# Unused full-width products beside the small products of the inverses' joining and of the sample sequences

## The chip, the cores and the metric

One Trainium2 chip, one of its cores. The metric is the device time of one execution in microseconds (us). The kernel before took 1914.19 us, the median of three runs (1911.26 to 1918.53).

## The reference

One inference step of a one-layer hybrid decoder trunk: 1024 prompt tokens and 8 sample sequences of 8 tokens, model width 1024. What matters here is the first of three parallel head groups, the RWKV-7 time mixing (8 heads of 64), a recurrence over tokens with a 64x64 state per head:

```python
def step(S, inp):
    r_t, w_t, k_t, v_t, a_t, b_t = inp
    sa = jnp.einsum('bhij,bhj->bhi', S, a_t)
    S = (S * w_t[:, :, None, :] + sa[..., None] * b_t[:, :, None, :]
         + v_t[..., None] * k_t[:, :, None, :])
    return S, jnp.einsum('bhij,bhj->bhi', S, r_t)
...
x = x + jnp.concatenate([y_a, y_b, y_c], axis=-1) @ w_out[l]
x = x + mem_attend(rms_norm(x, norm_mem_q[l]), mem_ks[l], mem_vs[l], mem_wq[l], mem_wo[l])
x = x + swiglu(rms_norm(x, norm_ffn[l]), ffn_w_up[l], ffn_w_down[l])
```

The other two head groups are a gated linear recurrence (RG-LRU) and a diagonal state-space model (S5). Everything is float32, and all outputs are compared: the activations, the new states of each group, and the keys and values of the 256 memory tokens.

## The kernel before

The tokens are split in two halves. Half 0 holds 512 prompt tokens and the 64 sample tokens, half 1 the other 512 prompt tokens. A large float32 product is done as three products of rounded parts (`mm3`, lines 173 to 179: high times high, L177, low times high, L178, high times low, L179). The small products are plain float32, which TensorE does in two passes, so a small product counts twice in the trace.

The recurrence is done in chunks of 64 tokens. In a chunk the recurrence becomes products with 64x64 matrices and one inverse of a unit triangular 64x64 matrix per head and chunk:

- `rwkv_operands(hf, gr)` makes the operands of half hf for two of the four head pairs and stores them in DRAM.
- `inverse(hf)` inverts all triangles of a half. VectorE inverts their 32x32 diagonal blocks, one matrix per partition (`unit_inverse`, 31 steps of two operations on the tiles `tm` and `Wu`, recorded at the helper's line L81). The blocks go through DRAM to the tile `WT`, and TensorE joins them: for each of two groups `gr`, 32 products of 32x32 from `TZ` and `XO` (first stage, L982), ScalarE copies the result to `TZ`, 32 products of 32x32 from `WT` and `TZ` (second stage, L988), ScalarE copies the result to `WT`.
- `Chunks.prep` makes masked products and transposes for two chunks (L1052, L1074, L1079), and `Chunks.chain` runs the recurrence itself, chunk after chunk (L1124, L1135, L1139, L1148, L1170). Each chunk needs the state of the one before. `Chunks.finish` normalises 256 tokens of the result: block sums on TensorE (L1193 of the tile `Y`, L1199 of `frs`), ScalarE and VectorE between them, then a store to DRAM (`yr`).
- `Chunks.sample_chain` does the 8 sample sequences. First, for each of two groups, 32 products with the old states (L1233, 64 partitions, 16 columns of result), then products of 64x64 (L1240 to L1263). L1275 updates the states at the end.

`C0` is the recurrence of half 0, `C1` that of half 1. Around them stand the products that feed other work: the keys and values of the memory tokens (`M.keys`, tiles `mh`, `ml`; `M.values`), the input projection of half 1 (tiles `HH`, `HL`), and later the output projection of half 0 (`w_out(0)`, tiles `yh`, `yl`, read from `yr`) and its queries (tiles `hqh`, `hql`).

The program is written in one order and put into another by a list scheduler, which works with estimated costs and with the priorities of lines 1643 to 1664 (`pr`, a larger number goes earlier). What it yields is one fixed order per engine. An instruction whose operands are late holds up all that stand behind it on its engine, but for weight loads of TensorE.

The results of the small products of the inverses, of `prep` and of `finish` go to two banks of PSUM in turn (`pct`, tag `pp`, `PPB` = 2). A new tile in a bank waits for the last reader of the old one:

```python
def pct(n="pp"):
    return pc.tile([P, 512], F32, name=n, tag="pp", bufs=PPB)
...
PPB, CHB, WTBUF = 2, 3, 1
```

Of the kernel before, what the change touches and what calls it, by code (L numbers as in the profile page):

```python
# [55 lines left out]
def body(tc, I, O, dbg=None):  # L56
    nc = tc.nc
    V, S, G, TE = nc.vector, nc.scalar, nc.gpsimd, nc.tensor
# [32 lines left out]
    def bc(ap, shape):  # L91
        return ap.to_broadcast(shape)
# [52 lines left out]
    def load_w(ap, shape=(P, 8, P)):  # L145
        raw = wp.tile(list(shape), F32, name="wr", tag="wr")
        ld(raw, ap)
        return wsplit(raw, list(shape))
# [62 lines left out]
    for hf, hp in ((0, hpA), (1, hpB)):  # L211
        w = W[hf] + (8 if hf == 0 else 0) + 1
# [20 lines left out]
    HB, LB = H[1]  # L233
# [56 lines left out]
    for i, (a, b, mus) in enumerate(LORA1):  # L290
        w = b - a
        raw = load_lora1(i) if i else first_w
        lmu = lp.tile([P, 8, P], F32, name="lmu", bufs=2) if i < 2 else raw[:, :, 32:64]
        for j, m in enumerate(mus):
            c = slice(64 * j, 64 * j + 64) if len(mus) == 2 else slice(0, w)
# [304 lines left out]
    for m in range(2):  # L600
        w = load_w(I['w_in'][16 + m])
# [33 lines left out]
    def th(n):  # L635
        return sp.tile([P, 512], F32, name="tsm", tag="th", bufs=2)[:, :n * P].rearrange("p (g c) -> p g c", c=P)
# [21 lines left out]
    for g in (slice(0, 4), slice(4, 8)):  # L658
        for ri, e0, e1, op in ((0, er, ei, OP.subtract), (1, ei, er, OP.add)):
            t, x = th(4), XX[:, ri, g, 1:129]  # L660
# [24 lines left out]
    for a, b in ((0, 3), (3, 6), (6, 8)):  # L685
        pvs = [smt()[:, :CW * 3].rearrange("p (g c) -> p g c", c=CW) for _ in range(2)]

        for h in range(2):
            for g in range(a, b):
                TE.matmul(pvs[h][:, g - a, :], toe[:, 2 * g + h, :], U[:, 2 * g + h, :], start=g == a, stop=False,  # L690
                          skip_group_check=True)
# [25 lines left out]
    for hf in range(2):  # L717
        for m in range(2):
            yo = sp.tile([P, W[hf]], F32, name="yo", tag="yo", bufs=2)
            for c0, n in GX[hf]:  # L720
                c = slice(OFF[hf] + c0, OFF[hf] + c0 + n)
# [221 lines left out]
    def pct(n="pp"):  # L943
        return pc.tile([P, 512], F32, name=n, tag="pp", bufs=PPB)

    def unit_inverse(Xt, Wt, nu, nb):

        Xv = Xt[:nu, :nb * nb].rearrange("p (s t) -> p s t", t=nb)
        Wv = Wt[:nu, :nb * nb].rearrange("p (s t) -> p s t", t=nb)
        G.memset(Wt[:nu, :nb * nb], 0.0)  # L950
        G.memset(Wt[:nu, 0:nb * nb:nb + 1], 1.0)
        tm = ip.tile([P, 256], F32, name="tm")
        for j in range(nb - 1, 0, -1):
            n = [nu, j, nb - j]
            tv = tm[:nu, :j * (nb - j)].rearrange("p (s t) -> p s t", s=j)
            tt(tv, bc(Xv[:, 0:j, j:j + 1], n), bc(Wv[:, j:j + 1, j:nb], n), OP.mult)
            tt(Wv[:, 0:j, j:nb], Wv[:, 0:j, j:nb], tv, OP.add)

    def inverse(hf):

        Xu, Wu = (ip.tile([P, 1024], F32, name=n, tag=n) for n in ("Xu", "Wu"))
        ld(Xu, inv_d[hf].rearrange("i p c s t -> (i p c) (s t)"))
        unit_inverse(Xu, Wu, P, 32)
        ld(inv_e[hf].rearrange("i p c s t -> (i p c) (s t)"), Wu)
        WT = iw.tile([P, 4, 8, 64], F32, name="WT", bufs=WTBUF)
        TZ, XO = (ip.tile([P, 4, 8, 32], F32, name=n, tag=t) for n, t in (("TZ", "Xu"), ("XO", "Wu")))
        for i in range(4):
            ld(WT[32 * i:32 * i + 32, :, :, 32 * (i % 2):32 * (i % 2) + 32].rearrange("s p c t -> s (p c) t"),
               inv_e[hf][i].rearrange("p c s t -> s (p c) t"))
        ab = [(slice(64 * h, 64 * h + 32), slice(64 * h + 32, 64 * h + 64)) for h in range(2)]  # L970
        for h, (a, b) in enumerate(ab):
            ld(XO[a], off_d[hf][h])
            G.memset(WT[b, :, :, 0:32], 0.0)
        for gr in range(2):
            g2 = slice(2 * gr, 2 * gr + 2)
            units = [(p, c, 32 * (8 * (p - 2 * gr) + c)) for p in range(2 * gr, 2 * gr + 2) for c in range(8)]
            for a, b in ab:
                V.transpose(TZ[a, g2].rearrange("p k c s -> p (k c) s"), WT[a, g2, :, 0:32].rearrange("p k c s -> p (k c) s"))
            pz = pct()
            for a, b in ab:  # L980
                for p, c, u in units:
                    TE.matmul(pz[b, u:u + 32], XO[a, p, c, :], TZ[a, p, c, :], start=True, stop=True)  # L982
            for a, b in ab:
                act(TZ[b, g2].rearrange("p k c s -> p (k c s)"), pz[b, :])
            pz = pct()
            for a, b in ab:
                for p, c, u in units:
                    TE.matmul(pz[a, u:u + 32], TZ[b, p, c, :], WT[b, p, c, 32:64], start=True, stop=True)  # L988
            for a, b in ab:
                act(WT[a, g2, :, 32:64].rearrange("p k c t -> p (k c) t"), pz[a].rearrange("p (c t) -> p c t", t=32))  # L990
        return WT
# [21 lines left out]
    class Chunks:  # L1013
# [201 lines left out]
        def sample_chain(self, ds, WT):  # L1215

            t = self.t
            S0 = t([P, 4, 8, 64], "AR", 2)
            ld(S0, I['wkv0'])
            CH = []  # L1220
            for gr in range(2):
                AR, SV = ds[gr]['AR'], ds[gr]['SV']
                s0 = S0[:, 2 * gr:2 * gr + 2]
                for h in range(2):
                    V.memset(SV[OWN[h], :, h, 0, :], 0.0)
                ch = self.ctile()
                CH.append(ch)
                for i in range(2):
                    for h in range(2):
                        o = OWN[h]  # L1230
                        for b in range(8):
                            c = slice(8 * b, 8 * b + 8)
                            TE.matmul(ch[o, 2:4, i, c], s0[o, i, b, :], AR[o, i, h, 0, 0:2, c], start=i == 0 and b == 0,  # L1233
                                      stop=False, skip_group_check=True)
                sa = t([P, 2, 64], "u0", 4)
                V.tensor_copy(sa, ch[:, 2])
                for i in range(2):
                    for h in range(2):
                        o = OWN[h]
                        TE.matmul(ch[o, 0, i], AR[:, i, h, 0, 0, :], SV[:, i, h, 0, :], start=False, stop=False,  # L1240
                                  skip_group_check=True)
                        TE.matmul(ch[o, 0, i], sa[o, i], c_('ident64')[o], start=False, stop=True, skip_group_check=True)
                for i in range(2):
                    for h in range(2):
                        TE.matmul(ch[OWN[h], 3, i], SV[:, i, h, 0, :], AR[:, i, h, 0, 1, :], start=False, stop=False,
                                  skip_group_check=True)
            for gr in range(2):
                ch, SV = CH[gr], ds[gr]['SV']
                u0 = t([P, 2, 64], "u0", 4)
                V.tensor_copy(u0, ch[:, 0])  # L1250
                for i in range(2):
                    for h in range(2):
                        o = OWN[h]
                        TE.matmul(ch[o, 1, i], WT[o, 2 * gr + i, :], u0[o, i], start=False, stop=True, skip_group_check=True)
                for h in range(2):
                    V.tensor_copy(SV[OWN[h], :, h, 0, :], ch[OWN[h], 1])
            ys = self.ytile()
            for gr in range(2):
                SV, XT, ch = ds[gr]['SV'], ds[gr]['XT'], CH[gr]
                for i in range(2):  # L1260
                    for h in range(2):
                        o = OWN[h]
                        TE.matmul(ch[o, 3, i], SV[o, i, h, 0, :], XT[o, i, 0, :], start=False, stop=True,  # L1263
                                  skip_group_check=True)
                act(ys[:, gr, :, :64], ch[:, 3])
            self.finish(512, 64, ys)
            for gr in range(2):
                SV, BKt, s0 = ds[gr]['SV'], ds[gr]['BKt'], S0[:, 2 * gr:2 * gr + 2]
                for i in range(2):
                    tt(s0[:, i], s0[:, i], bc(pcs[0][:, 2 * gr + i, 8:16, None], [P, 8, 64]), OP.mult, G)  # L1270
                    cs = pct()
                    for h in range(2):
                        svm = t([P, 8, 64], "hat")
                        tt(svm, bc(SV[:, i, h, 0, None, :], [P, 8, 64]), bc(c_('rmask')[:, :, None], [P, 8, 64]), OP.mult, G)
                        TE.matmul(cs[OWN[h], :], BKt[:, i, 0, h, :], svm.rearrange("p b j -> p (b j)"), start=True, stop=True)  # L1275
                    tt(s0[:, i], s0[:, i], cs.rearrange("p (b j) -> p b j", b=8), OP.add)
            ld(O['wkv_s'], S0)
# [356 lines left out]
    M = Memory()  # L1634
# [2 lines left out]
        return tc.high_priority(offset=d)  # L1637

    mm_ = [mmt]
    C0 = Chunks(0, L_)  # L1640
    WS = sample_inverse()
    C0.run_sample(WS)
    with pr(1500):
        WTA = inverse(0)
    rwkv_operands(1, 0)
    M.load()
    with pr(300):
        C0.run(WTA)
    M.keys(range(0, 4))
    rwkv_operands(1, 1)  # L1650
    with pr(800):
        WTB = inverse(1)
    with pr(800):
        M.values(0)
    with pr(2500):
# [7 lines left out]
    with pr(2500):  # L1663
        C1.run(WTB)
    C0.es.close()
    M.es.close()
# [373 lines left out]
```

## Time and profile before

| what | value |
|---|---|
| median of 3 runs | 1914.19 us (1911.26 to 1918.53) |
| the profiled execution | 1913.72 us, its span 1911.9 us |
| TensorE (PE) busy | 1783.5 us (93% of the span) |
| VectorE (DVE) busy | 1110.3 us (58%) |
| ScalarE (ACT) busy | 791.6 us (41%) |
| GpSimd (POOL) busy | 706.1 us (37%) |
| mean granted clock of TensorE | 0.955 of full speed |

The span is what the profiler sees of an execution, and the execution took 1.8 us more. Busy time includes time at the half clock: TensorE has two levels, 2.4 GHz (shown as 1.00) and 1.2 GHz (0.50), and a mean between them over a stretch says how much of it lay at either. The small products in question lie between 360 and 390 us (sample sequences), 447 and 464 us (joining for half 0) and 655 and 672 us (joining for half 1).

### The profile page before, as it was taken

Reading aid. Unit: us, or ns where it says so; the run is one execution under the profiler, and the core shown is the slowest. Engines: PE = TensorE matmul, PEld = TensorE weight load, DVE = VectorE, ACT = ScalarE, POOL = GpSimd, SP = SyncE. Lnnn points to the kernel's source line nnn. Section 1 sums busy time; section 2 is a strip of 40 time slices with the busy share of each in tenths; the row PEclk is TensorE's granted clock in tenths of the full one; section 3 lists DMA queues with packets and bytes.
Section 4 is the critical chain, followed back from the end, with each engine's and each line's share of the span. In section 5 each row is a group of like instructions: output and inputs, shape, how many; then the busy total and the mean of one; then the engine's idle time right before and its main releaser. Section 6 shows DMA issues by size and latency. Waiting matters only on the chain.

```text
span 1911.9 us, 34508 instructions
## 1 busy us (share of the span) xinstructions
PE 1783.5 (93%) x13640; PEld 1621.8 (85%) x13640; DVE 1110.3 (58%) x2259; ACT 791.6 (41%) x1465; POOL 706.1 (37%) x523
## 2 busy tenths in 40 slices
PE   6998898989999999999998986999999999999997
PEld 6878787768877788797888976999999999999997
DVE  7764776797779454647755597533333332744435
ACT  8442443453434533434645355433333333411114
POOL 3311323344443423323231345644444443522235
PEclk9999998798998989999999997999999999999998
DMA  5136456437554752255553341322222213822102
GB/s 164 30 118 142 125 154 155 127 95 199 152 147 122 229 160 71 80 170 190 170 177 122 122 148 57 111 78 70 91 68 80 72 66 114 278 91 92 57 1 94
DMA packets 185426, 228.94 MB, mean 120 GB/s; under 512 B 78961, under 2 KB 127473, under 8 KB 184849
## 3 DMA queue, kind: packets, MB, share of 16 engines
q1 hardware_dynamic: 185264, 226.74, 39.0%
q8 instruction: 107, 1.75, 0.4%
q14 instruction: 55, 0.44, 0.1%
HBM read 170.47 MB, written 56.23 MB: 119 GB/s over the span
## 4 chain that ended last, share of the span: by engine, by line
PE 60%; DVE 11%; DMA 5%; issue 4%; POOL 2%; ACT 2%; SPq 1%; DVEq 0%; ACTq 0%; POOLq 0%
PE mm L179 17%; PE mm L177 17%; PE mm L178 17%; DVE Wu L81 1%; DVE tm L81 1%; DVE Y L78 1%; DMA AR<-ar 1%; DMA fg<-g 1%; PE pp L1052 1%; POOL wl L81 1%; DMA raw<-yr 1%; DVE h L78 1%; DVE bl L81 1%; ACT L75 1%; PE ss L1487 1%
## 5 line engine op out<-in xcount | busy, mean ns | idle before, releaser
L81 POOL TENSOR_TENSOR wl<-wr,wh 128x1024 fp32r<-128x1024 f32 x100 | 245.5, 2456 | 451.9 <-ACT wh L75 389.1
L177 PE MATMUL mm<-bh,st 128*128 128x288 f32 (+1 forms) x640 | 185.5, 292 | 5.3 <-ACT p L75 2.5
L177 PE MATMUL mm<-HH,wh 128*128 128x256 f32 (+2 forms) x576 | 180.9, 314 | 10.1 <-ACT Y L75 3.8
L179 PE MATMUL mm<-bh,st 128*128 128x288 f32 (+1 forms) x640 | 186.7, 293 | 1.5 <-POOL st L81 1.1
L178 PE MATMUL mm<-bl,st 128*128 128x288 f32 (+1 forms) x640 | 186.2, 292 | 0.0
L177 PE MATMUL mm<-bh,X 128*128 128x256 f32 (+1 forms) x592 | 170.6, 290 | 10.3 <-ACT X L75 10.3
L81 DVE TENSOR_TENSOR X<-X,mm 128x288 f32<-128x288 f32 (+2 forms) x200 | 100.5, 513 | 137.0 <-PE mm L179 136.2
L179 PE MATMUL mm<-gh,dl 128*128 128x288 f32 (+2 forms) x560 | 178.8, 320 | 0.2 <-POOL dl L81 0.2
L177 PE MATMUL mm<-gh,dh 128*128 128x288 f32 (+2 forms) x560 | 178.3, 318 | 0.0
L178 PE MATMUL mm<-gl,dh 128*128 128x288 f32 (+2 forms) x560 | 178.3, 318 | 0.0
L179 PE MATMUL mm<-HH,wl 128*128 128x256 f32 (+2 forms) x576 | 177.4, 308 | 0.0
L75 ACT ACTIVATE wh<-wr 128x1024 fp32r<-128x1024 f32 (+1 forms) x101 | 106.2, 1051 | 171.5 <-PE mm L178 96.8
L178 PE MATMUL mm<-HL,wh 128*128 128x256 f32 (+2 forms) x576 | 175.7, 305 | 0.0
L179 PE MATMUL mm<-bh,X 128*128 128x256 f32 (+1 forms) x592 | 171.0, 290 | 2.3 <-POOL X L81 2.3
L178 PE MATMUL mm<-bl,X 128*128 128x256 f32 (+1 forms) x592 | 170.8, 289 | 0.0
L81 DVE TENSOR_TENSOR gy<-gy,mm 128x256 f32<-128x256 f32 (+1 forms) x132 | 57.6, 437 | 175.6 <-PE mm L179 171.0
L177 PEld LDWEIGHTS mm<-HH,wh 128*128 128x128 f32 x576 | 115.8, 201 | 17.8 <-issue 6.7
L177 PEld LDWEIGHTS mm<-bh,st 128*128 128x128 f32 x640 | 122.3, 192 | 6.5 <-ACT p L75 2.8
L179 PEld LDWEIGHTS mm<-bh,st 128*128 128x128 f32 x640 | 122.7, 192 | 3.1 <-POOL st L81 2.8
L81 POOL TENSOR_TENSOR dl<-wr,dh 128x512 fp32r<-128x512 f32 x44 | 64.3, 1491 | 164.2 <-ACT dh L75 141.9
L178 PEld LDWEIGHTS mm<-bl,st 128*128 128x128 f32 x640 | 122.8, 192 | 0.1
L177 PEld LDWEIGHTS mm<-bh,X 128*128 128x128 f32 x592 | 112.4, 191 | 10.8 <-ACT X L75 10.8
(479 smaller groups left out, 5082.3 us busy)
## 6 DMA issues: line engine op xcount, KB each, us to landing
wr<-in_w_in SPq DMA_DIRECT2D x34, 512.0 KB, 4.0
X<-in_w_up SPq DMA_DIRECT2D x32, 512.0 KB, 3.5
wr<-in_w_down SPq DMA_DIRECT2D x22, 512.0 KB, 3.9
wr<-in_w_out SPq DMA_DIRECT2D x16, 512.0 KB, 5.3
wr<-in_wq SPq DMA_DIRECT2D x16, 512.0 KB, 3.6
kvb<-in_ck SPq DMA_DIRECT2D x32, 256.0 KB, 4.4
kvb<-in_cv SPq DMA_DIRECT2D x32, 256.0 KB, 4.2
wr<-in_wo SPq DMA_DIRECT2D x16, 512.0 KB, 3.5
```

The source lines that it names most:

```text
L75: return S.activation(out, in_, f, **kw)
L78: return V.scalar_tensor_tensor(out, a, s, b, op0=o0, op1=o1)
L81: return (eng or V).tensor_tensor(out, a, b, op=op)
L177: paced(TE.matmul(out, wh, xh, start=first and k == 0, stop=False, **kw))
L178: paced(TE.matmul(out, wh, xl, start=False, stop=False, **kw))
L179: paced(TE.matmul(out, wl, xh, start=False, stop=last and k == n - 1, **kw))
L1052: mi = TE.matmul(pvs[h][:, i, j], BK[o, i, j].rearrange("p a t -> p (a t)"), AR[o, i, h, j].rearrange("p a t -> p (a t)"), start=True, sto ...
L1487: TE.matmul(sc[32 * h:32 * h + 32, :256], qp[:, 2 * h + dt, :], kb[:, dt, :], start=dt == 0, stop=dt == 1)
```

## The change

A helper `full` writes one product with a 128x128 stationary and a 128x512 moving operand to a bank of `pct`. Nothing reads the result. `inverse` takes a function that gives the operands. It takes its PSUM tile one step ahead (`after`), and writes one full product to that tile before each of the four blocks of 16 small products of a group, so 8 for each inverse. `sample_chain` takes one tile (`side`) and writes one full product before each of its 8 blocks of 8 small products at L1233. That is 24 full products. Their operands are in SBUF long before: for half 0 and the samples the normalised input (`HB`), for half 1 the memory tokens (`M.h`). The lines below the edit move down by up to 16, so that L982 becomes L989, L988 L996, L1052 L1060, L1074 L1082, L1079 L1087, L1124 L1132, L1170 L1178, L1193 L1201, L1199 L1207, L1233 L1243, L1240 L1250, L1242 L1252 and L1275 L1285. The full products are at L948.

```diff
+    def full(bank, w, x):
+
+        return TE.matmul(bank, w, x, start=True, stop=True, skip_group_check=True)
+
...
-    def inverse(hf):
+    def inverse(hf, fill):
...
+        after = pct()
         for gr in range(2):
...
-            pz = pct()
+            pz, after = after, pct()
             for a, b in ab:
+                full(after, *fill())
                 for p, c, u in units:
                     TE.matmul(pz[b, u:u + 32], XO[a, p, c, :], TZ[a, p, c, :], start=True, stop=True)
             for a, b in ab:
                 act(TZ[b, g2].rearrange("p k c s -> p (k c s)"), pz[b, :])
-            pz = pct()
+            pz, after = after, pct()
             for a, b in ab:
+                full(after, *fill())
                 for p, c, u in units:
                     TE.matmul(pz[a, u:u + 32], TZ[b, p, c, :], WT[b, p, c, 32:64], start=True, stop=True)
...
             CH = []
+            side = pct()
             for gr in range(2):
...
                         o = OWN[h]
+                        full(side, *hfill())
                         for b in range(8):
...
+    def hfill():
+        return HB[:, 0, 1:129], HB[:, 1, 1:513]
+
+    def mfill():
+        return M.h[0][:, 0, 0:128], M.h[1].rearrange("p k c -> p (k c)")
+
...
-        WTA = inverse(0)
+        WTA = inverse(0, hfill)
...
-        WTB = inverse(1)
+        WTB = inverse(1, mfill)
```

The scheduler gives a new order, on all engines, from the sample sequences on. Three places of TensorE's order follow. A row that ends in x22 stands for 22 instructions. `pp` are the tiles of `pct`, `ch` those of the chains, `mm` and `bs` those of the large products and of the block sums.

The sample sequences, in the kernel before, from the last of the products with the old states on:

```order
L1233 MATMUL ch<-AR 64x2x8 x22
L1074 MATMUL pp<-C_ident,hat 128x128 x2
L1233 MATMUL ch<-AR 64x2x8 x11
L179 MATMUL mm<-HH,wl 128x256
L177 MATMUL mm<-HH,wh 128x256
L178 MATMUL mm<-HL,wh 128x256
L1079 MATMUL pp<-C_ident,vt 64x128 x2
L1240 MATMUL ch<-SV,AR 64x64
```

The same place in the changed kernel:

```order
L1243 MATMUL ch<-AR 64x2x8 x22
L1082 MATMUL pp<-C_ident,hat 128x128 x2
L1243 MATMUL ch<-AR 64x2x8 x11
L179 MATMUL mm<-HH,wl 128x256
L177 MATMUL mm<-HH,wh 128x256
L178 MATMUL mm<-HL,wh 128x256
L1087 MATMUL pp<-C_ident,vt 64x128 x2
L1250 MATMUL ch<-SV,AR 64x64
L1252 MATMUL ch<-C_blk,u_3674 64x64
L1250 MATMUL ch<-SV,AR 64x64
L948 MATMUL pp<-HH 128x512 x4
L1252 MATMUL ch<-C_blk,u_3674 64x64
```

All 64 products of L1243 still stand before the first full product, in the same order. Four full products stand here, the other four (2 and 2) within the next dozen rows.

The joining for half 0, in the kernel before (21 large products stand here in a row, of which the first is shown):

```order
L1275 MATMUL pp<-hat,BKt 64x512
L982 MATMUL pp<-TZ,XO 32x32 x32
L764 MATMUL bs<-zz,C_blk 128x512
L177 MATMUL mm<-mh,wh 128x256
...
L1275 MATMUL pp<-hat,BKt 64x512
L988 MATMUL pp<-WT,TZ 32x32 x32
L177 MATMUL mm<-mh,wh 128x256
L178 MATMUL mm<-ml,wh 128x256
L982 MATMUL pp<-TZ,XO 32x32 x32
L179 MATMUL mm<-mh,wl 128x256
L988 MATMUL pp<-WT,TZ 32x32 x32
```

In the changed kernel:

```order
L948 MATMUL pp<-HH 128x512 x2
L178 MATMUL mm<-ml,wh 128x256
L179 MATMUL mm<-mh,wl 128x256
L1285 MATMUL pp<-hat,BKt 64x512
L989 MATMUL pp<-TZ,XO 32x32 x32
L996 MATMUL pp<-WT,TZ 32x32 x13
L948 MATMUL pp<-HH 128x512
L996 MATMUL pp<-WT,TZ 32x32 x3
L948 MATMUL pp<-HH 128x512
L996 MATMUL pp<-WT,TZ 32x32 x16
L989 MATMUL pp<-TZ,XO 32x32 x32
L948 MATMUL pp<-HH 128x512 x2
```

The 21 large products no longer stand between the first stage and the second, but behind the joining. No full product stands within a first stage, and two within each second stage.

The end of C0 and the beginning of the joining for half 1, in the kernel before, from the block sums of the second group of `finish` on (24 large products stand here in a row, of which the first is shown):

```order
L1193 MATMUL pp<-Y,C_blk 128x256 x2
L177 MATMUL mm<-mh,wh 128x256
...
L1199 MATMUL pp<-frs,C_blk 128x256
L982 MATMUL pp<-TZ,XO 32x32 x32
L1199 MATMUL pp<-frs,C_blk 128x256
```

In the changed kernel (left out are 23 large products):

```order
L1201 MATMUL pp<-Y,C_blk 128x256 x2
L177 MATMUL mm<-mh,wh 128x256
L178 MATMUL mm<-ml,wh 128x256
L1207 MATMUL pp<-frs,C_blk 128x256
L948 MATMUL pp<-mh 128x512 x2
L1207 MATMUL pp<-frs,C_blk 128x256
...
L989 MATMUL pp<-TZ,XO 32x32 x32
```

The last block sums of C0 have moved ahead of 23 large products and of the first stage of the joining, and only two large products stand between them and the sums that they build on.

## Rows read from the trace of the kernel before

**Rows 1.** The page: span, TensorE, its granted clock in 40 slices.
```profile
span 1911.9 us, 34508 instructions
PE 1783.5 (93%) x13640; PEld 1621.8 (85%) x13640; DVE 1110.3 (58%) x2259; ACT 791.6 (41%) x1465; POOL 706.1 (37%) x523
PEclk9999998798998989999999997999999999999998
```
**Rows 2.** Busy time by stretch: from:to, length, busy us (instructions) per engine, PEclk, DMA share, GB/s.
```profile
365.00:386.00 21.00, 21.00 (x147) 16.67 (x146) 18.87 (x56) 5.72 (x10) 7.05 (x4) 0.51 0.25 68
386.00:420.00 34.00, 31.21 (x228) 25.71 (x226) 33.01 (x72) 18.90 (x26) 12.58 (x7) 1.00 0.28 85
420.00:430.00 10.00, 5.42 (x33) 3.82 (x31) 9.15 (x18) 6.31 (x6) 7.12 (x6) 1.00 0.40 139
437.00:457.00 20.00, 20.00 (x262) 16.40 (x262) 13.30 (x20) 4.63 (x7) 9.76 (x7) 1.00 0.84 209
457.00:468.00 11.00, 10.84 (x145) 10.14 (x141) 6.49 (x6) 7.42 (x11) 7.35 (x5) 0.53 0.53 198
665.00:669.00 4.00, 4.00 (x23) 3.78 (x22) 2.13 (x5) 1.07 (x3) 0.03 (x1) 0.58 0.48 144
672.00:682.00 10.00, 7.34 (x44) 5.72 (x44) 3.18 (x7) 3.08 (x8) 1.60 (x2) 0.52 0.93 295
```
**Rows 3.** Busy time by stretch of TensorE alone, where its clock falls.
```profile
365.00:366.00 1.00, 1.00 (x13) 0.64 0.00 0
```
**Rows 4.** Timeline of TensorE, joining for half 0: start, length, line, operands, count, [idle before].
```profile
447.63 2.11 PE L982 MATMUL pp<-TZ,XO 32*32 32x32 f32 x64
...
454.23 2.11 PE L988 MATMUL pp<-WT,TZ 32*32 32x32 f32 x64
...
456.70 2.95 PE L982 MATMUL pp<-TZ,XO 32*32 32x32 f32 x64
...
460.33 3.43 PE L988 MATMUL pp<-WT,TZ 32*32 32x32 f32 x64 [0.17 <-ACT TZ L75]
```
**Rows 5.** Timeline of TensorE: neighbours of 512 columns, then neighbours of 256 columns.
```profile
639.94 0.39 PE L179 MATMUL mm<-wh,ml 128*128 128x512 f32 x1
640.17 0.40 PE L177 MATMUL mm<-wh,mh 128*128 128x512 f32 x1
...
466.17 0.41 PE L179 MATMUL mm<-HH,wl 128*128 128x256 f32 x1
466.38 0.42 PE L177 MATMUL mm<-HH,wh 128*128 128x256 f32 x1
```
**Rows 6.** Timeline of ScalarE: copies between the stages of the joining, half 0, half 1.
```profile
459.69 1.20 ACT L75 ACTIVATE TZ<-pp 32x512 f32<-32x512 f32 x2 [2.13 <-PE pp L982]
...
657.24 1.19 ACT L75 ACTIVATE TZ<-pp 32x512 f32<-32x512 f32 x2 [0.84 <-PE pp L982]
658.45 0.69 ACT L75 ACTIVATE frs<-pp,kc 128x512 f32<-128x512 f32 x1
```
**Rows 7.** Timeline of TensorE: end of C0, joining for half 1, start of w_out(0).
```profile
647.96 1.13 PE L1199 MATMUL pp<-frs,C_blk 128*128 128x256 f32 x4 [1.14 <-ACT frs L75]
...
654.57 0.59 PE L1199 MATMUL pp<-frs,C_blk 128*128 128x256 f32 x2
655.09 2.11 PE L982 MATMUL pp<-TZ,XO 32*32 32x32 f32 x64
657.13 0.70 PE L1199 MATMUL pp<-frs,C_blk 128*128 128x256 f32 x2
...
682.19 0.85 PE L177 MATMUL mm<-yh,wh 128*128 128x288 f32 x2 [0.97 <-ACT yh L75]
```
**Rows 8.** Timeline of TensorE: end of C1, start of the attention and of w_out(1).
```profile
826.98 1.03 PE L1199 MATMUL pp<-frs,C_blk 128*128 128x256 f32 x4
...
862.23 0.50 PE L177 MATMUL mm<-yh,wh 128*128 128x512 f32 x1
```
**Rows 9.** Timeline of ScalarE: the operands of w_out(1) arrive.
```profile
855.63 1.99 ACT L75 ACTIVATE yh<-raw 128x512 fp32r<-128x512 f32 x3 [5.30 <-DMA raw<-yr]
```

## The prediction

> **What bounds the kernel now.** I read the page first. TensorE is busy 93% of the span, and the slices of its granted clock show where it did not run at full speed: in the first half of the span and in one spot behind it [rows 1]. What TensorE does therefore sets the time, except where it waits or where another engine is as full. The busy times by stretch tell which of these holds at the three places of the change [rows 2]. Between 365 and 386 us, in the sample sequences, TensorE is busy all of the 21.00 us, at a clock of 0.51. VectorE is full there too, 18.87 of 21 us, and 33.01 of 34 us in the stretch behind it, with the inversion of the 32x32 blocks. At 420 to 430 us TensorE is busy only 5.42 of 10 us, while VectorE still is 9.15. So up to 430 us VectorE sets the pace. At 437 to 457 us TensorE is busy 20.00 of 20 us, and from 457 to 468 us it is busy 10.84 of 11 at a clock of 0.53. That is the joining for half 0, and there TensorE is the limit. At the joining for half 1 the clock is low at 665 to 669 us, and at 672 to 682 us, where TensorE is idle for 2.7 us as well.
>
> The timeline shows what the low clock is: a first stage of the joining takes 2.11 us at full speed, the last second stage 3.43 us [rows 4].
>
> **The sum, against the profiled execution's 1913.7 us** (span 1911.9; the median of the runs, 1914.2, is 0.5 higher, which I leave out).
>
> *The price of one full product.* Two neighbours of 512 columns start 0.23 us apart at full clock, two of 256 columns 0.21 us apart at half clock [rows 5], which makes 0.42 us for 512 columns at half clock.
>
> *The samples: 0.* Eight products at half clock are 8 x 0.42 = 3.4 us. What hides them is VectorE's inversion up to 430 us, and the 4.6 us for which TensorE is idle just before [rows 2]. With that cover gone they cost 3.4 us.
>
> *Joining for half 0: +2.6.* TensorE has no idle time there. Two products stand ahead of the small ones, the rest among them, where the clock was falling: 4 x 0.23 + 4 x 0.42 = 2.6 us, between 1.8 (all at full clock) and 3.4.
>
> *Its order: +1.1.* In the new order a second stage stands right behind its first stage, and must wait for ScalarE's two copies, 1.2 us [rows 6]. Before, 21 large products stood between the first pair, and the only wait that the row shows is 0.17 us [rows 4]. Two such waits make 2.2 us more idle time (2.4 less 0.2). The large products are still to be done and can fill a later gap, so between 0 and 2.2; I take half, 1.1.
>
> *Joining for half 1: +1.8.* Eight products at full clock, 8 x 0.23 (3.4 at half).
>
> *The end of C0: -2.* The last block sums of `finish` no longer stand behind the first stage of the joining (2.11 us) and 23 large products (0.12 us each, half of 0.23, together 2.8 us) [rows 5, 7], and ScalarE's work on them not behind the copies of the joining (1.19 us) [rows 6]. On this path, which ends with the first product of `w_out(0)` at 682.19 us, that is up to 6.1 us. But all of this work still has to be done by TensorE, so what can be had is its idle time there, the 2.7 us between 672 and 682 [rows 2] and the 0.97 us ahead of `w_out(0)` [rows 7]. Against that, the sums now wait for ScalarE with two or three large products as cover. Before, with 24 in front, the wait was 1.14 us [rows 7]; with 21 fewer it is 1.14 + 21 x 0.12 = 3.7 us. Bounds -6.1 and +7.4 (two such waits); I take -2, nearer to the idle time that the trace shows than to the waits, because the rest of the row's path, through DMA, is untouched.
>
> *The end of C1: +1.4.* The chain of C1 ends later: counted in the order, 219 large products stood between its last block sums and the first of the attention, now 160. From the end of those sums (828.0 us) to the first product of `w_out(1)` (862.23) [rows 8] lay these 219 and 12 of the attention, 34.2 us or 0.148 us each, waits included. Now 172 give 25.5 us. The operands were complete for the third tile 28.3 us after the sums (855.63 + 0.66 - 828.0) [rows 9], and the six products of the first two tiles take 6 x 0.23 = 1.4 us. That leaves 28.3 - 25.5 - 1.4 = 1.4 us of waiting, between 0 and 2.8.
>
> *The clock: 0.* This is the term that decides. What the half clock costs is read from the stretches: (1 - 0.53) x 11 = 5.2 us for half 0, (1 - 0.58) x 4 = 1.7 and (1 - 0.52) x 10 = 4.8 us for half 1, together 11.7 us that could be won where TensorE is the limit. In the samples it is (1 - 0.51) x 21 = 10.3 us, but there VectorE sets the pace. I take nothing, for two reasons. First, the order: in the samples the products with the old states all run before the first full product, and the clock fell in their midst, at 365 us [rows 3], so that fall stays. In the joining a first stage still has no full product in it. Second, the amount: two full products are 0.46 us beside 2.11 us of small ones, and the 0.24 us of large products that stood between the two stages at 456 us did not keep the clock from falling [rows 4]. Bounds 0 and -11.7, or -22 with the samples.
>
> The Trainium skill, "TensorE: Matmul & The Clock Gate", section "Why this matters for your kernels", speaks against the change in another way: by it the clock falls after an idle gap between bursts of products, so that a stretch of small products without a gap keeps it, and full products there add work and win nothing. By that rule the sum would be the same and the upside of 11.7 us would not exist. The trace differs: the clock falls to 0.64 in a microsecond in which TensorE was busy for 1.00 of 1.00 us [rows 3], so I keep the upside as a rival.
>
> Sum: 0 + 2.6 + 1.1 + 1.8 - 2 + 1.4 + 0 = +4.9, so **1918.6 us**, 0.2% above the median. A measurement of this kernel can tell about 0.5% (9.6 us) from no change, so this forecast is "no change".
>
> **The rivals.**
>
> *The clock stays up.* The full products are just enough for both joinings. For it: each second stage now has two full products in it, where nothing but small ones stood, and `w_out(0)` follows the joining for half 1 more closely. Against it: their small share. The time: 1913.7 + 1.8 + 1.8 + 1.1 - 2 + 1.4 - 11.7 = 1906; with half of the samples' 10.3 us as well, if VectorE's new order lets TensorE set the pace there, 1901.
>
> *The wait for the block sums takes over (slower).* At the end of C0 TensorE now stands in line behind `frs` with hardly any cover. If both waits are 3.7 us and nothing is won back, the term is +7.4 in place of -2: 1928. It decides where these waits exceed the idle time that they replace, 2.7 + 0.97 us. For it: TensorE takes its instructions in order, and the wait of 1.14 us was there even with cover. Against it: the path behind it gets shorter by as much.
>
> *Only the order counts.* The products themselves change nothing, since most of them don't stand where the edit puts them, and the new order alone moves the time by some microseconds either way. That lies within the forecast's range and has its chance there.
>
> **How the numbers follow.** The forecast and its neighbourhood get 0.50, the clock that stays up 0.24, the wait for the block sums 0.22, and 0.04 is left for what I don't see. Faster by over 0.5% means below 1904.6: most of the second case, as half of the samples comes with it, and a little of the rest, 0.21. Slower by over 0.5% means above 1923.8: the third case and the upper end of the first, 0.26. The rest is 0.53. The range goes from 1900, the faster rival with the samples, to 1931, the slower rival with the joinings' products at half clock (3.4 for 2.6 and 3.4 for 1.8, +2.4).
>
> **What would show it.** In the profile after: the granted clock falls at the products with the old states as before, and is near 0.5 for some 10 us at the joining for half 0; a wait for ScalarE of about 1 us stands ahead of the second stages; the full products start 0.23 or 0.42 us apart; the first product of `w_out(0)` comes within 5 us of 682; TensorE waits ahead of L1207 for ScalarE. I am wrong if the clock is 1.00 through both joinings, or if the time ahead of 700 us stays the same and the difference arises behind it.

## The result, and the profile after

The kernel after takes 1934.89 us, the median of four runs (1932.73 to 1937.78), against 1914.64 us for the kernel before on the same chip (1911.26 to 1918.53). The ratio is 1.0112, with a 95% interval from 1.0086 to 1.0138: slower by 20 us, beyond the predicted range, on the side that had a chance of 0.26.

The page of the kernel after, the lines that answer to [rows 1]:

```profile
span 1930.9 us, 34551 instructions
PE 1788.9 (93%) x13664; PEld 1621.8 (84%) x13664; DVE 1104.4 (57%) x2259; ACT 792.0 (41%) x1467; POOL 710.4 (37%) x523
PEclk9999998797999889999999998999999999999998
```

The span is 19.0 us longer, but TensorE is busy for only 5.4 us more (1788.9 against 1783.5). The other 13.6 us are time in which it waits: 1930.9 - 1788.9 = 142.0 us of idle time, 128.4 before. So the 24 products, and what the clock made of them and of everything else, come to 5.4 us. The rest is waiting. Against the kernel before, this waiting lies ahead of 670 us (89.8 us of idle time there, 76.7 before; from 670 to 1070 us 17.5 and 16.1). Experiment 2 shows why the time is nevertheless not lost there for good.

The timeline of TensorE in the kernel after, at the samples and at the joining for half 0, answers to [rows 4] (L1243 are the products with the old states, L948 the full products, L989 and L996 the two stages):

```profile
371.85 2.13 PE L1243 MATMUL ch<-AR 64*64 64x16 f32 x22
...
376.48 2.08 PE L948 MATMUL pp<-HH 128*128 128x512 f32 x4
...
452.40 0.73 PE L948 MATMUL pp<-HH 128*128 128x512 f32 x2
...
455.50 2.11 PE L989 MATMUL pp<-TZ,XO 32*32 32x32 f32 x64 [0.78 <-DVE zb L743]
...
458.29 1.00 PE L996 MATMUL pp<-WT,TZ 32*32 32x32 f32 x26 [0.68 <-ACT TZ L75]
459.22 0.53 PE L948 MATMUL pp<-HH 128*128 128x512 f32 x1
...
460.13 0.80 PE L948 MATMUL pp<-HH 128*128 128x512 f32 x1
...
465.73 1.22 PE L948 MATMUL pp<-HH 128*128 128x512 f32 x2
...
681.91 0.50 PE L948 MATMUL pp<-mh 128*128 128x512 f32 x1
```

In the samples the first full product comes behind the last small one, so nothing is interleaved there. In the joining two of them do stand inside each second stage. A pair takes 0.73 us at full clock and 1.22 us at half clock; a single one took 0.50 us at full clock (the last row, from the joining for half 1) and 0.80 us at half clock, so neighbours are 0.23 and 0.42 us apart, the prices that were predicted.

Busy time by stretch of TensorE in the kernel after (length, busy time, granted clock, DMA share, GB/s): the whole stage of the joining for half 0 up to the chain, then two stretches ahead of the joining for half 1:

```profile
455.00:489.00 34.00, 32.78 (x387) 0.70 0.77 229
648.00:654.00 6.00, 2.41 (x32) 0.73 0.31 117
664.00:672.00 8.00, 3.76 (x14) 0.95 0.55 175
```

The clock is lower than before over the joining for half 0 (0.70 against 0.83, the latter in the rows of experiment 4). TensorE is idle for 3.6 of 6 us and 4.2 of 8 us shortly before the joining for half 1, which the timeline explains (rows that answer to [rows 7]):

```profile
652.49 0.69 PE L1143 MATMUL ch<-u,WT 64*64 64x64 f32 x8 [3.22 <-DVE u L1136]
...
664.55 1.13 PE L1207 MATMUL pp<-frs,C_blk 128*128 128x256 f32 x4 [1.03 <-ACT frs L75]
...
670.22 0.39 PE L177 MATMUL mm<-mh,wh 128*128 128x256 f32 x1 [3.67 <-ACT wh L75]
...
676.57 2.11 PE L989 MATMUL pp<-TZ,XO 32*32 32x32 f32 x64
...
698.69 0.85 PE L177 MATMUL mm<-yh,wh 128*128 128x288 f32 x2
```

The joining for half 1 begins 21.5 us later than before, `w_out(0)` 16.5 us later. Neither of the two long waits is for anything that the edit touches: one is for VectorE's copy of `u` in the chain of half 0, the other for a weight that ScalarE rounds (and ScalarE sat idle for the last 1.36 us before it, until the weight's transfer had landed). (The first products of `prep` begin 2.4 us later too, ahead of the whole change. So much does one profile differ from another, and less is not read from them here.)

### The profile page after: what moved, and what is told of

Same layout as the page of the kernel before. It is cut to its first block, busy times and chain, and to the rows that moved or that the text cites. A ratio compares the mean times of both kernels' runs of the same rounds, so it can differ in the third digit from the quotient of the medians.

```text
span 1930.9 us, 34551 instructions
## 1 busy us (share of the span) xinstructions
PE 1788.9 (93%) x13664; PEld 1621.8 (84%) x13664; DVE 1104.4 (57%) x2259; ACT 792.0 (41%) x1467; POOL 710.4 (37%) x523
## 4 chain that ended last, share of the span: by engine, by line
PE 68%; DVE 16%; DMA 5%; ACT 4%; issue 4%; POOL 2%; SPq 1%; DVEq 0%; ACTq 0%; POOLq 0%
PE mm L179 18%; PE mm L177 18%; PE mm L178 18%; DVE Wu L81 2%; DVE tm L81 1%; ACT L75 1%; PE pp L1060 1%; DVE Y L78 1%; DMA AR<-ar 1%; DVE tsm L81 1%; DVE zz L78 1%; DVE h L78 1%; DVE bl L81 1%; PE bs L764 1%; PE ch L1132 1%
## 5 line engine op out<-in xcount | busy, mean ns | idle before, releaser
L177 PE MATMUL mm<-HH,wh 128*128 128x256 f32 (+2 forms) x576 | 177.0, 307 | 12.0 <-DVE ext L81 7.7
```

Of the source, the lines that this page charges most:

```text
L177: paced(TE.matmul(out, wh, xh, start=first and k == 0, stop=False, **kw))
```

## The experiments

**1. Are these the products, or the order?** The scheduler put the whole program into a new order, so two kernels separate the two. In the first the order is that of the kernel after and the products are shortened once it is fixed; in the second the order is that of the kernel before and the products are put in once it is fixed.

```diff
+def resize(nc, n):
+    for blk in nc.main_func.blocks:
+        for k, i in enumerate(blk.instructions):
+            if i.name in FULL:
+                x, w = i.ins
+                blk.instructions[k] = i.__replace__(ins=[cut(x, n), w], outs=[cut(i.outs[0], n)])
...
         body(tc, I, O)
+    resize(nc, 64)
```

> The kernel after with its order kept, instruction for instruction, on every engine; only the 24 full products are cut from 512 to 64 columns once the order is fixed (their results are used by nothing). Theory order (the scheduler's new order costs the 20 us, the products only their own run time): 24 products lose 7/8 of 0.21 to 0.43 us each, 4.5 to 9 us if all of it lay on TensorE's path and about 3 to 5 with what stands beside VectorE's waits, so 1929 to 1932 us. Theory products (the full products, with what queues behind them and a longer stretch of low clock, cost the 20 us): 1915 to 1920 us.

Measured: 1932.07 us, ratio 1.0084 (1.0068 to 1.0100). The long wait is there again, in the timeline of TensorE of this kernel:

```profile
651.72 0.69 PE L1143 MATMUL ch<-u,WT 64*64 64x64 f32 x8 [3.22 <-DVE u L1136]
```

In the kernel before, ahead of the first small product of each sample group (4) and of each stage of a joining (2):

```diff
+                for j in range(n):
+                    new.append(i.__replace__(name=nc.get_next_instruction_name(), ins=list(ops[src]), outs=[full], tile_size=(128, 128), tile_position=(0, 0),
...
             new.append(i)
```

> The kernel before with its order kept on every engine; the 24 full products of 512 columns are put in once the order is fixed, ahead of the first small product of each block (4 for each of the two sample groups, 2 for each stage of the joining), into the bank that the block then overwrites, so no other bank is held. Theory order: only their run time where TensorE is what is waited for, the 16 of the joining at 0.21 to 0.43 us: 1917 to 1922 us. Theory products: near the kernel after, 1930 to 1936 us. Rival clock (the products lift the granted clock of the stages around them): 1900 to 1910 us.

Measured: 1917.67 us, ratio 1.0022 (1.0006 to 1.0037). So in the old order the products alone cost 4.2 us (1.1 to 7.1). In the new order cutting them to an eighth gains 0.28%, 5 us, which agrees but is not clear of noise. With them cut, the new order is still 16 us slower than the kernel before. The order is the cause of most of the loss. "Order" takes in here what the edit does to the banks of `pct`, in which `after` (in each joining) and `side` take one more tile: the first kernel keeps that, the second has none of it, and no run parts it from the order.

**2. Parts of the change.** Each leaves out `full` in one or two of the three places (samples, joining for half 0, joining for half 1):

```diff
-        WTA = inverse(0, hfill)
+        WTA = inverse(0, None)
...
-                full(after, *fill())
+                full(after, *fill()) if fill else None
```

> Only the 8 full products of the sample sequences, the joining as before; the scheduler makes its own order of it. Theory order: the program is put into another order from the samples on, and the time can move by many times the 8 products' own 1.7 to 3.4 us, either way: somewhere in 1905 to 1935, with no tie to how many products were added. Theory products: 8 of 24, 1914 to 1921 us.

> Only the 16 full products of the two joinings, the samples as before; the scheduler makes its own order of it. Theory order: 1905 to 1935 us, not tied to the count of products. Theory products: 16 of 24, 1925 to 1930 us, and with the run before it this adds up to the 20 us of the whole change.

> Only the 8 full products of the joining of half 0. Theory order: a new order of its own from that joining on, time somewhere in 1900 to 1930 us. Theory products: 8 of 24, with the whole cost of the first joining in it, 1918 to 1924 us.

> Only the 8 full products of the joining of half 1; the order up to 650 us stays that of before. Theory order: it can only move what comes after, so the time stays nearer to before than in the other partial runs, 1908 to 1922 us, and the granted clock up to 650 us is that of before. Theory products: 8 of 24, 1917 to 1924 us.

> The products of the samples and of the joining of half 0, none at the joining of half 1: the order of the kernel after up to its second joining (some 640 us), another order from there on. Theory early order (the part of the order up to the second joining, which starts 21 us late in the kernel after, sets the loss): 1926 to 1936 us. Theory late order (the part behind it does): 1895 to 1918 us.

> The products of the samples and of the joining of half 1, none at the joining of half 0: the order of the kernel with the sample products alone (1895 us) up to its second joining, another from there on. Theory early order: 1890 to 1900 us. Theory late order: 1905 to 1925 us.

| products at | us | ratio to before (95%) |
|---|---|---|
| none (before) | 1914.6 | 1 |
| samples | 1895.28 | 0.9891 (0.9873 to 0.9910) |
| half 0 | 1894.89 | 0.9890 (0.9863 to 0.9917) |
| half 1 | 1907.96 | 0.9971 (0.9948 to 0.9994) |
| samples, half 0 | 1912.82 | 1.0007 (0.9989 to 1.0024) |
| samples, half 1 | 1905.96 | 0.9965 (0.9952 to 0.9977) |
| half 0, half 1 | 1917.15 | 1.0015 (0.9999 to 1.0030) |
| all three (after) | 1934.89 | 1.0112 (1.0086 to 1.0138) |

Each ratio is to the kernel before on the same chip, whose median lay between 1912.5 and 1914.6 us; differences between rows are taken from the ratios. All four ranges that theory products gave are missed on the fast side. Theory order gave no tie to the number of products, which holds, but its ranges were too narrow as well: the samples and half 0 came out 10 and 5 us below theirs, half 1 at the very edge. Of the last two runs both lie where theory late order had them. Each part alone makes the kernel faster, by 6 to 21 us, and all of them together make it 20 us slower. No price per product fits that. The parts don't add up; each is a new draw of the order.

The table also says where the loss of the kernel after lies. It shares its order with the kernel of samples and half 0 up to the second joining (TensorE's two traces have the same sequence up to 671 us), and that one is no slower than before. So the order from the second joining on makes the 20 us between the two. The same step (from half 0 to half 0 and half 1) costs 24 us, and 14 us from samples to samples and half 1, but from none to half 1 it gains 6 us.

What this step did is seen in the page of the kernel of samples and half 0, in its timeline of TensorE (second joining, first product of `w_out(0)`, first product of the queries of half 0, last read-out of the chain C1), and in the timeline of the kernel after (the last two of these, the others being shown above, and two waits behind them).

```profile
span 1914.0 us, 34535 instructions
PE 1785.4 (93%) x13656; PEld 1622.5 (85%) x13656; DVE 1118.1 (58%) x2259; ACT 791.6 (41%) x1467; POOL 709.5 (37%) x523
```

```profile
672.53 2.81 PE L989 MATMUL pp<-TZ,XO 32*32 32x32 f32 x64
...
706.55 0.54 PE L177 MATMUL mm<-yh,wh 128*128 128x288 f32 x2 [0.97 <-ACT yh L75]
...
809.11 0.40 PE L177 MATMUL mm<-hqh,wh 128*128 128x288 f32 x1
...
825.26 0.45 PE L1178 MATMUL ch<-XT,SV 64*64 64x64 f32 x8
```

```profile
796.87 0.38 PE L177 MATMUL mm<-hqh,wh 128*128 128x288 f32 x1 [0.31 <-DVE X L81]
...
842.32 0.45 PE L1178 MATMUL ch<-XT,SV 64*64 64x64 f32 x8
...
880.90 0.50 PE L177 MATMUL mm<-yh,wh 128*128 128x512 f32 x1 [1.45 <-ACT yh L75]
...
1038.90 0.50 PE L177 MATMUL sc<-kh,qh 128*128 128x256 f32 x2 [3.82 <-ACT kh L75]
```

In the kernel of samples and half 0 the second joining begins at 672.53 us, nearly as late as in the kernel after, and `w_out(0)` even at 706.55 us, 24 us later than before and 8 us later than in the kernel after, and yet it loses nothing against the kernel before: being late there is not yet a loss. Of the 16.9 us between these two spans 13.4 are idle time of TensorE (142.0 against 128.6). Where they arise is seen in TensorE's busy time from 780 to 1070 us, in the kernels before, after, of samples and half 0, of half 0, and of half 0 and half 1:

```profile
780.00:1070.00 290.00, 280.65 (x2013) 0.98 0.47 150
780.00:1070.00 290.00, 273.95 (x1980) 0.98 0.45 145
780.00:1070.00 290.00, 284.00 (x2100) 1.00 0.49 157
780.00:1070.00 290.00, 285.70 (x2070) 1.00 0.49 157
780.00:1070.00 290.00, 275.81 (x1966) 0.98 0.46 150
```

That is 16.0 us of idle time in the kernel after against 6.0 with samples and half 0, and 14.2 with half 0 and half 1 against 4.3 with half 0, each time with a lower clock as well. The two other kernels that share the order of the kernel after have 16.5 us (experiment 1) and 16.6 us (experiment 5) there, so this belongs to the order. Ahead of 670 us the idle time of one order differs by up to 6 us from one execution to the next (89.8, 84.2 and 83.5 us in the kernel after, with samples and half 0, and with the shortened products), so not all of the 13.4 us can be put down to the order.

In the kernel after, the chain C1 ends 17 us later than with samples and half 0, while the queries, large products that could have stood beside it, begin 12 us earlier. What follows then waits, in small pieces. The pair of half 0, and half 0 with half 1, differs in the same way: the last read-out starts at 803.0 and 823.3 us, the queries at 786.8 and 780.0. That this shift is what costs the time is read from the traces; no run changed it by itself. Waits for a bank of `pct` don't follow the loss: those of `prep`'s transposes (L1082) for VectorE's `AR`, which reads the old tile, come between 350 and 900 us to 6.8 us in the kernel after and 3.2 us before, but to 8.6 us with samples and half 0 and to 1.9 us with half 0 and half 1.

**3. How much does an order alone move?** The kernel of the samples with its order kept and its products cut to 64 columns (the `resize` of experiment 1), and the kernel before with a single product of 64 columns more:

```diff
+            side = pct()[:, 0:64]
...
+                        full(side, *hfill()) if gr == i == h == 0 else None
```

> The kernel with only the sample products, its order kept on every engine; the 8 full products cut from 512 to 64 columns once the order is fixed. Theory order: the 19 us that this kernel gained come from the order alone, so 1892 to 1898 us again. Rival clock (the 8 wide products themselves lift the granted clock): without them the gain goes, 1908 to 1916 us.

> The kernel before with one single product added, 64 columns wide, in the sample chain (and the bank of results that it writes to); the scheduler makes its own order of it. Its own run time is under 0.1 us. Theory order: a quarter of TensorE's instructions stand elsewhere, so the time moves by 5 to 25 us either way, out of the interval of the kernel before. Theory products: 1912 to 1917 us.

Measured: 1891.13 us, ratio 0.9876 (0.9851 to 0.9902), and 1902.66 us, ratio 0.9960 (0.9945 to 0.9976). The gain of the sample products stays without them. One product that costs next to nothing, with the bank that it takes, moves the time by 0.4%. The kernel of the samples shows what a better order gains (its page, its busy time of TensorE by stretch, and the same two stretches of the kernel before):

```profile
span 1893.5 us, 34513 instructions
PE 1766.9 (93%) x13648; PEld 1605.2 (85%) x13648; DVE 1111.9 (59%) x2259; ACT 792.5 (42%) x1467; POOL 710.7 (38%) x523
```

```profile
480.00:550.00 70.00, 69.02 (x754) 1.00 0.57 154
650.00:700.00 50.00, 46.00 (x591) 0.97 0.69 217
```

```profile
480.00:550.00 70.00, 65.28 (x686) 0.93 0.53 140
650.00:700.00 50.00, 45.14 (x529) 0.80 0.56 180
```

With eight products more, TensorE is busy for 16.6 us less, of 18.4 us of span. The clock stays up in the chain of half 0 and through the joining for half 1, where there is no full product at all.

**4. Can full products hold the clock?** In the old order, with more of them ahead of each sample group and each stage (the second run has `n *= 2`, and the joinings alone):

```diff
     for names, src, n in Beside.plan:
+        n *= 4
```

> As the run with the products put into the old order, but four times as many: 16 ahead of each sample group, 8 ahead of each stage of the joining, 96 in all. Theory order, with products that only cost their run time: 96 at 0.21 to 0.43 us are 20 to 41 us, less what stands beside VectorE's waits in the sample stage; from 1915 us that gives 1928 to 1948 us, and the granted clock of the small products' stages stays as it was. Rival clock (enough wide products hold the clock up through the small ones): the low stretches of 10 to 18 us at the samples and joinings shrink, which gives back up to 20 us: 1915 to 1925 us.

> The old order, with products at the joinings alone, 4 ahead of each stage (32 in all, against 2 and 16 in the change). With 8 ahead of each stage the granted clock stayed at its upper level through both joinings. Theory threshold (4 are enough to hold it): 32 at 0.21 us are 6.8 us, and the low stretches of 10 and 18 us at the joinings, worth half of their busy time, come back: 1907 to 1914 us. Rival (4 are not enough): 1917 to 1923 us.

Measured: with 8 ahead of each stage and 16 ahead of each sample group 1923.92 us, ratio 1.0054 (1.0038 to 1.0070), in the range of the rival; with 4 ahead of each stage and none at the samples 1911.18 us, ratio 0.9990 (0.9977 to 1.0003), in the range of theory threshold. The busy time of TensorE from a joining's first stage to the chain or to `w_out(0)`, for half 0 and half 1: before, then with 2, 4 and 8 products ahead of each stage.

```profile
448.00:479.00 31.00, 29.80 (x396) 0.83 0.72 199
655.00:682.00 27.00, 23.98 (x353) 0.76 0.67 207
```

```profile
456.00:488.00 32.00, 31.64 (x407) 0.84 0.73 203
664.00:693.00 29.00, 26.75 (x358) 0.72 0.66 217
```

```profile
450.00:483.00 33.00, 31.40 (x415) 0.95 0.72 192
659.00:687.00 28.00, 25.75 (x365) 0.85 0.67 216
```

```profile
460.00:494.00 34.00, 31.67 (x422) 1.00 0.58 167
669.00:699.00 30.00, 27.55 (x378) 0.91 0.59 188
```

In the joining for half 0 two do nothing (0.83 to 0.84), four help (0.95), and with eight the clock does not fall. In the joining for half 1 two don't help either (0.76 and 0.72), and with eight the clock stays up for the 21 us in which TensorE is busy throughout; it is lower behind them (0.69 from 690 to 699 us, where TensorE is busy for 6.55 of 9 us):

```profile
669.00:690.00 21.00, 21.00 (x329) 1.00 0.50 158
```

But they pay no more than they cost: 32 products are 32 x 0.23 = 7.4 us, and the time is that of before. With 96, the 72 that are more than in experiment 1 are 16.6 us at full clock. The pages have TensorE busy for 1.1 us more than in experiment 1 (first row: 24 products, second row: 96):

```profile
PE 1788.1 (94%) x13664; PEld 1624.1 (85%) x13664; DVE 1111.6 (58%) x2259; ACT 790.2 (41%) x1465; POOL 708.1 (37%) x523
PE 1789.2 (93%) x13736; PEld 1623.3 (84%) x13736; DVE 1112.4 (58%) x2259; ACT 791.0 (41%) x1465; POOL 707.0 (37%) x523
```

So the clock gave back some 15 us of TensorE's busy time, and the kernel still took 6 us more: its idle time is 8.6 us longer (132.9 against 124.3 us, with spans of 1922.1 and 1912.4 us). What it waits for there was not looked into.

**5. Is it VectorE, ahead of the joining for half 1?** In the kernel after more of the inversion stands among the copies that the chain waits for. (The counts in the first expectation, 40 and 22, are those of stretches that end some 22 and 5 us ahead of the joining. In the last 50 us ahead of its first product it is 23 operations with 11.3 us, against 13 with 5.8 us in the kernel before.) Both kernels with these operations cut:

```diff
-            tt(tv, bc(Xv[:, 0:j, j:j + 1], n), bc(Wv[:, j:j + 1, j:nb], n), OP.mult)
+            one = tt(tv, bc(Xv[:, 0:j, j:j + 1], n), bc(Wv[:, j:j + 1, j:nb], n), OP.mult)
...
+            if i.name in THIN:
+                blk.instructions[k] = i.__replace__(ins=[one(p) for p in i.ins], outs=[one(p) for p in i.outs])
```

> The kernel after with its order kept; the 62 operations of VectorE that invert the diagonal blocks of half 1 (tiles tm and Wu) are cut to one element per partition once the order is fixed, so the inverse of half 1 is left out. In the kernel after 40 of them (22 us) stand in the last 50 us before the joining of half 1, among the copies that the chain of half 0 waits for; in the kernel before 22 (9 us). Theory VectorE (the new order lays the inversion beside the chain's end, and this costs a good part of the 20 us): 6 to 12 us less than the kernel after, 1922 to 1929 us. Rival spread (the loss lies in many small places of the order): 1930 to 1935 us.

> The same cut in the kernel before, order kept. Theory VectorE: there the inversion stands beside fewer of the chain's copies, so at most 3 us less, 1911 to 1915 us. Rival: the inversion is on the path in both kernels, and this run gains as much as the one of the kernel after, 1902 to 1908 us.

Measured: 1925.36 us, ratio 1.0060 (1.0039 to 1.0082), and 1904.91 us, ratio 0.9952 (0.9931 to 0.9973). The first lies in the range of theory VectorE, the second in that of the rival. The cut gains 0.52% in the kernel after and 0.48% in the kernel before. The inversion is on the path in both, by about as much, so it is not what tells them apart; with these intervals a difference of up to some 8 us between the two gains can't be excluded. What speaks against the theory besides is the kernel of samples and half 0: its inversion stands in the same place (25 operations, 13.9 us, in the last 50 us), and it is no slower than the kernel before.

## Why the prediction was wrong

**The products: right.** The sum had 0 + 2.6 + 1.8 = 4.4 us for them; in the old order, where those of the samples stand elsewhere, they cost 4.2 us (1.1 to 7.1). The prices of 0.23 and 0.42 us stand in the trace as forecast.

**The clock: right in the sum.** The forecast was no gain, because two products are too few and because those of the samples run behind the small ones. Both are seen: 0.84 for 0.83 with two in the old order, and the first L948 of the samples at 376.48 us. Over the whole span the mean granted clock is 0.957, 0.955 before. By places it moved: the joining for half 0 ran at 0.70 over 34 us in place of 0.83 over 31 us, which is some 5 us lost and lies outside the bounds of 0 and -11.7, and other places gave it back. The rival that the clock stays up is out for this change, though with eight products its mechanism is real. The Trainium skill's rule that was cited against it ("TensorE: Matmul & The Clock Gate", "Why this matters for your kernels": idle gaps lower the clock) would have had full products win nothing in any number. For the clock the runs with four and eight differ from it (0.95 and 1.00 against 0.83); for the time it came out so, as the clock gave back no more than the products cost.

**The order: this is the step that failed.** The prediction priced the order by three places near the edit: the second stage behind its first (+1.1), the end of C0 (-2) and the end of C1 (+1.4), together +0.5 us, and put the rest of the new order at nothing. Measured is 1934.89 - 1917.67 = 17.2 us. At the three places themselves it was off by 2 us at most. ScalarE's copies hold up one of the two second stages, for 0.68 us (two waits of 1.2 us were the upper bound); within `w_out(1)` TensorE waits 1.45 us for `yh` (1.4 forecast). The end of C0 is as long as before: from the first block sums behind `frs` to `w_out(0)` it is 34.1 us (664.55 to 698.69) against 34.2 us (647.96 to 682.19), so about 0 in place of -2. That `w_out(0)` begins at 698.69 us, not within 5 us of 682, was lateness from further ahead. And the prediction took that start for the end of a path whose delay is a delay of the kernel: with samples and half 0 it comes at 706.55 us, in a kernel that loses nothing.

The rival for that place, a wait for the block sums of up to 3.7 us, rests on a misread row: the 1.14 us before stand ahead of the first group's sums (647.96 us), while the sums with 24 large products in front (654.57 us) wait for nothing in the trace. In the kernel after, the wait ahead of the first group's sums is 1.03 us. So the rival guessed the right side for a reason that the trace does not show. (The range's upper end, 1931, is 1928 + 2.4 = 1930.4.)

What the sum left out is that 13.6 of the 19.0 us of span are waits, hardly any of them at an edited line, and that which order catches up behind the second joining (experiment 2) is decided far from the edit. Neither of the two signs that the prediction named for being wrong came: the clock is not 1.00 through the joinings, and the time ahead of 700 us did not stay the same.

**"Only the order counts": the right mechanism, mis-sized.** The prediction has it as a rival that moves the time "by some microseconds either way" and lies within the forecast's range. It moved it by -23 us (the shortened samples) to +16 us (the shortened products of the whole change). Of the eight new orders measured here, those of the table and that of the single small product, five are faster than the kernel before, two can't be told from it, and only that of the change itself is slower. So nothing in the mechanism led to the slow side; that this change drew the slowest of the eight orders is chance.

## What to carry to other kernels

Where a list scheduler sets the order, price an edit twice: what the instructions cost in the old order, and how far orders of the same program differ. The second was four times the first here (17.2 against 4.2 us), and a harmless edit, or one product more, measures it cheaply. A gain of 1% from an edit whose work can be cut away without losing the gain is a gain of the order: the fastest kernel here (1891.13 us) came about that way, and its order is worth keeping, not the products.

## What the runs showed of the hardware

TensorE's clock depends on what stands ahead of small products, not on idle time alone: [rows 3] and experiment 4 show it falling while TensorE was busy throughout, and staying up with eight wide products ahead of each stage. Ahead of [rows 3] TensorE had been busy without a gap, at the upper level, in the kernel before:

```profile
358.50:365.00 6.50, 6.50 (x87) 1.00 0.19 76
```

A multiplication of VectorE took 2.65 us in place of 0.69 while GpSimd was splitting weights. The rows are VectorE's timeline and GpSimd's in the kernel after; the last is from the list of the tile `gz` in the kernel before (shortest, median and longest in ns).

```profile
649.58 2.65 DVE L81 TENSOR_TENSOR gz<-gz,hs 128x512 f32<-128x512 f32 x1
652.15 0.28 DVE L1136 COPY u<-ch 128x128 f32<-128x128 f32 x1
```

```profile
648.61 5.83 POOL L81 TENSOR_TENSOR wl<-wr,wh 128x1024 fp32r<-128x1024 f32 x2 [4.84 <-ACT wh L75]
```

```profile
L81 DVE TENSOR_TENSOR gz<-gz,hs x2: 680/686/693, 618.5 to 635.8; 128x512 f32<-128x512 f32 x2
```

This is 2 us of the wait of 3.22 us for `u`. The Trainium skill ("SBUF — State Buffer", "SBUF: two separate sides") says that such an operation of VectorE with two inputs in SBUF and one of GpSimd exclude each other for a whole instruction; the trace agrees, as 2.65 us is 0.69 and some 2 us of a split that takes GpSimd 2.46 us in the mean. It is not the cause of the 20 us: the kernel of samples and half 0 has the same 2.65 us and is no slower than before.
